# A third seven-product pair in the double gate blocks of a decoder layer, with more buffers around it and the background weight loads at other rates

## The chip, the cores and the metric

The kernel runs on one core of one Trainium2 chip. The metric is the device time of one launch in microseconds (us). TensorE (PE) multiplies 128x128 weights by 128x512 blocks, VectorE (DVE) and ScalarE (ACT) prepare operands and read results, SyncE's queue (SP) issues nearly all DMAs. PSUM has eight banks of 128x512 fp32; the kernel uses four as `acc` and four as `misc`.

## The reference

One decoder layer, T = 256 tokens, D = 2048, feed-forward width 5632, all fp32:

```python
mod = silu(c) @ w_ada + b_ada                 # shift1, scale1, gate1, shift2, scale2, gate2
h = rms_norm(x, norm1_gain) * (1 + scale1) + shift1
proj = h @ w_in                               # q, k, v of three mixers, r_gla, a_gla, gate_cols
g = sigmoid(gate_cols.reshape(b, t, 3, d))    # three branch gates of 2048 columns each
y = g[:, :, 0] * (o_sb @ w_br_sb) + g[:, :, 1] * (o_dil @ w_br_dil) + g[:, :, 2] * (o_gla @ w_br_gla)
x = x + gate1 * (y @ w_out)
h = rms_norm(x, norm2_gain) * (1 + scale2) + shift2
x = x + gate2 * swiglu(h, w_ffn_in, w_ffn_out)
```

The mixers o_sb, o_dil and o_gla (stick-breaking, dilated and gated linear attention) are small beside the weight products.

## The kernel before, in words

**Products.** Every fp32 product is made of three: the left factor and the weight are each split into a high part (rounded to fp32r) and a low remainder, and `mm3` (L172 to L175) multiplies high by high, high by low and low by high into one bank. Weights come as raw tiles of 512 KB (`raw`, L151 in `load_weights`, L216 in `load_pair`). ACT casts the high half `whi` (L165, L236), DVE subtracts it from the raw tile to give `wlo` (L166, L222). One such pair of halves is a "room". Rooms and raws are rings of four, longer where a stage gives further tags (`more_rooms`, `more_raws`); tags such as X1, A9, T0, ada are fixed pieces of SBUF used by one stage after another.

**Places.** A double block of output (two blocks of 512 columns for both halves of 128 tokens: four banks) is computed by `fast_products` in eight places, each of 256 rows of the weights. A plain place costs 8 x 3 = 24 matmuls and two splits of 128x1024 on DVE. A place marked 1 is a seven-product pair (Strassen's scheme): 7 x 3 = 21 matmuls, but DVE makes three splits of 128x1024, one of 128x512 and four differences of 128x512. It needs sums of the left factors (`sums_of_h`) and four further banks for the products that are shared between outputs. After the last fast place DVE combines those four banks (L316 to L319), and `merge` adds the combinations to the four outputs (L273).

**Stages.** After the input projection come, in order: `gate_block(0, br)` for three branches (one block of 512 gate columns each), three `gate_pair`s (double blocks 1 and 2 of the gates of each branch), the transposes of the GLA output, which stand in PE's order just ahead of the first pair and whose results are read on DVE at L1263, the `y_block`s 0 to 2 (the branch projections times the gates), the last gate blocks and `y_block(3)`, the output projection with `w_out` in four blocks n of 512 columns, and the feed-forward part. The residual of block n of the output projection loads a tile of x (L1424, `A<-x`), multiplies the bank by gate1 (L1347, which is the last reader of the bank) and adds (L1348).

**Background.** The rows of `w_ada` for later modulation vectors are streamed in meanwhile: a generator issues one load of 512 KB per step and a multiply-accumulate on DVE (L424). `tick(rate)` advances it by `rate` steps every second 128-row slice of the weights. The rates are constants at the top (`RATE_PAIRS` for the gate pairs, `RATE_Y`, `RATE_LAST`, `RATES_OP`).

**What sets the order.** The code is recorded, and a scheduler orders each engine's instructions by priorities (`prio`) and its own estimate of the times. Every engine then runs its own list strictly in that order, and waits at an instruction until its semaphores are there.

Of the kernel before, what the change touches and what calls it, by code (L numbers as in the profile page):

```python
# [10 lines left out]
F32 = mybir.dt.float32  # L11
# [6 lines left out]
P = 128  # L18
T = 256
# [10 lines left out]
N_DIL = 6  # L30
N_GLA = 4
SEG_SHIFT1, SEG_SCALE1, SEG_GATE1, SEG_SHIFT2, SEG_SCALE2, SEG_GATE2 = range(6)
RATE_IN, RATE_MID, RATE_GATES, RATE_PAIRS, RATE_Y, RATE_LAST = 0.8, 0.6, 0.65, 0.42, 0.5, 0.7

RATES_OP, RATES_FFN, RATE_OUT = (0.85, 0.5, 0.0), (0.75, 0.9, 0.7, 0.6), 0.5
GATE2_CUT = 12
LOOK = 3
DEFER = 4
# [11 lines left out]
OUT_B = ((0, 0), (1, 0)) + tuple(x for a, b in zip((8, 9, 10, 11, 12, 13, 6, 7), (2, 3, 4, 5, 14, 15, 16, 17)) for x in ((a, 1), (b, 0)))  # L50
PAIRS = ((0, 0), (1, 0), (5, 1), (2, 0), (6, 1), (7, 1), (3, 0), (4, 0))
PAIRS_4 = ((0, 0), (1, 0), (4, 1), (5, 1), (2, 0), (6, 1), (7, 1), (3, 0))
GATE_PAIRS = ((0, 0), (1, 0), (4, 1), (2, 0), (3, 0), (5, 1), (6, 0), (7, 0))
FOUR = (2, 3, 5, 6, 8)
RANK = 16
ROW_N1, ROW_N2, ROW_SBQ, ROW_SBK, ROW_DILQ, ROW_DILK, ROW_GB, ROW_GG = 16, 32, 48, 49, 50, 51, 52, 56
# [24 lines left out]
def trunk(ctx: ExitStack, tc: tile.TileContext, I, out):  # L81
# [16 lines left out]
    def S(tag, shape, dtype=F32):  # L98
        return slot.tile(shape, dtype, tag=tag, name=nm(tag))
# [101 lines left out]
    def sums_of(sf, h, a, b):  # L201

        (a0, b0), (a1, b1) = ((x[:, a, :], x[:, b, :]) for x in h)
        for dst, x, y, op in (
            (0, a1, b1, ALU.add), (2, a0, a1, ALU.subtract), (1, sf[:, 0], a0, ALU.subtract), (3, b0, sf[:, 1], ALU.subtract)
        ):
            nc.vector.tensor_tensor(sf[:, dst], x, y, op=op)

    def load_pair(src, p, c0, c1, fast, tags):


        def raw_at(c):
# [3 lines left out]
            nc.sync.dma_start(raw, src[2 * p * P : (2 * p + 2) * P, c : c + NB].rearrange("(k p) c -> p k c", p=P))  # L216
            return raw

        def sub(dst, x, y):
            chain = state.get("chain")  # L220
            with tc.issue_after(chain.ins) if chain is not None else nullcontext():
                done = nc.vector.tensor_tensor(dst, x, y, op=ALU.subtract)  # L222
            if "chain" in state:
                state["chain"] = done
            return done

        def split(src):
            n = src.shape[1]
            more_rooms = state.get("more_rooms", ())
            i = state["tiles"] = (state.get("tiles", -1) + 1) % (4 + len(more_rooms))  # L230
            if i < len(more_rooms):
                hi, lo = (S(tag, [P, 2, NB], F32R) for tag in more_rooms[i])
            else:
                hi = wp.tile([P, 2, NB], F32R, tag="whi", name=nm("whi"), bufs=4)
                lo = wp.tile([P, 2, NB], F32R, tag="wlo", name=nm("wlo"), bufs=4)
            nc.scalar.copy(hi[:, :n, :], src)  # L236
            state["split"] = sub(lo[:, :n, :], src, hi[:, :n, :].bitcast(F32))
            return [(hi[:, i, :], lo[:, i, :]) for i in range(n)]

        with prio():  # L240
            if not fast:
                return [split(raw_at(c0)), split(raw_at(c1))]
            r0, r1 = raw_at(c0), raw_at(c1)
            b11, b21 = split(r0)
            ta, tb = (S(tag, [P, 2, NB]) for tag in tags)
            sub(ta[:, 0], r1[:, 0], r0[:, 0])
            sub(ta[:, 1], r1[:, 1], r1[:, 0])
            (b22,) = split(r1[:, 1:2])
            sub(tb[:, 0], r1[:, 1], ta[:, 0])
            sub(tb[:, 1], r0[:, 1], tb[:, 0])  # L250
            t1, t3 = split(ta)
            t2, t4 = split(tb)
            return b11, b21, b22, t1, t3, t2, t4
# [955 lines left out]
                gates[1 + i, br] = g  # L1209

    def sums_of_h():
        j = 2
        full = S("X1", [P, 4, T])
        nc.vector.tensor_tensor(full, hT[0][j].bitcast(F32), hT[1][j].bitcast(F32), op=ALU.add)
        sf = S("X2", [P, 4, 2, P])
        sums_of(sf, [full[:, :, t * P : (t + 1) * P] for t in range(NT)], slice(0, 4, 2), slice(1, 4, 2))
        hi, lo = (S(tag, [P, 4, 2, P], F32R) for tag in ("T1", "T2"))
        nc.scalar.copy(hi, sf)
        nc.vector.tensor_tensor(lo, sf, hi.bitcast(F32), op=ALU.subtract)
        return {2 * j + m: [(hi[:, i, m, :], lo[:, i, m, :]) for i in range(4)] for m in range(2)}  # L1220

    with prio():
        groups = dil_weights()
# [3 lines left out]
    ring["tags"] = ("AR0", "AR1", "KC", "KD")  # L1227
    od, turns = mixture(groups[0])
    gate_block(0, 1, turns)
    gate_block(0, 2)  # L1230


# [431 lines left out]
```

## Time and profile before

| | us |
|---|---|
| median of three runs (1577.26, 1577.41, 1579.7) | 1577.41 |
| the profiled execution, its own time | 1576.77 |
| span of its trace | 1575.0 |
| granted TensorE clock in it | 0.999 |
| PE busy / DVE busy / ACT busy, of the span | 99% / 89% / 56% |

In the trace a row gives start, duration, engine, line and operation with output and inputs by the program's names; in brackets stands how long the engine had been idle and what released it. Durations of neighbouring rows overlap a little, so what an operation costs in a row of many is the distance of the starts. "PE" is the matmul and "PEld" the load of its weights, which runs beside it. In the trace the gate pairs run from 490.89 to about 620 us, the output projection from about 777 to 869 us.

### The profile page before, as it was taken

Reading aid. Unit: us, or ns where it says so; the run is one execution under the profiler, and the core shown is the slowest. Engines: PE = TensorE matmul, PEld = TensorE weight load, DVE = VectorE, ACT = ScalarE, POOL = GpSimd, SP = SyncE. Lnnn points to the kernel's source line nnn. Section 1 sums busy time; section 2 is a strip of 40 time slices with the busy share of each in tenths; the row PEclk is TensorE's granted clock in tenths of the full one; section 3 lists DMA queues with packets and bytes.
Section 4 is the critical chain, followed back from the end, with each engine's and each line's share of the span. In section 5 each row is a group of like instructions: output and inputs, shape, how many; then the busy total and the mean of one; then the engine's idle time right before and its main releaser. Section 6 shows DMA issues by size and latency. Waiting matters only on the chain.

```text
span 1575.0 us, 20266 instructions
## 1 busy us (share of the span) xinstructions
PE 1563.4 (99%) x7186; PEld 1293.5 (82%) x7186; DVE 1394.3 (89%) x1704; ACT 876.9 (56%) x1215; POOL 12.6 (1%) x24
## 2 busy tenths in 40 slices
PE   8999999999999999999999999999999999999998
PEld 7878888888888788888888888888888888888887
DVE  6889996888888899987977888999999999899896
ACT  5654448875765545444435645556555555455553
POOL 1000000000000000000000000000000000000000
PEclk9999999999999999999999999999999999999999
DMA  9999997677787888989998886665666566876764
GB/s 333 361 326 323 336 308 239 221 237 224 240 293 256 269 290 273 316 255 320 305 329 258 299 301 205 188 212 188 201 203 211 174 201 231 291 229 202 222 212 136
DMA packets 196317, 402.26 MB, mean 255 GB/s; under 512 B 13102, under 2 KB 28116, under 8 KB 196216
## 3 DMA queue, kind: packets, MB, share of 16 engines
q1 hardware_dynamic: 194952, 397.75, 76.5%
q0 software_dynamic: 1088, 3.16, 0.5%
q8 instruction: 56, 0.92, 0.2%
q14 instruction: 45, 0.37, 0.1%
q10 hardware_dynamic: 176, 0.07, 0.0%
HBM read 395.68 MB, written 5.24 MB: 255 GB/s over the span
## 4 chain that ended last, share of the span: by engine, by line
PE 91%; DVE 4%; DMA 2%; ACT 2%; issue 1%; SPq 0%; DVEq 0%; ACTq 0%
PE acc L175 21%; PE acc L174 21%; PE acc L173 21%; PE misc L174 7%; PE misc L175 7%; PE misc L173 7%; DVE wlo L222 1%; PE acc L579 1%; PE misc L948 1%; DVE A L222 1%; PE misc L1287 1%; DVE T L424 0%; DVE wlo L166 0%; DMA A<-x 0%; PE misc L572 0%
## 5 line engine op out<-in xcount | busy, mean ns | idle before, releaser
L165 ACT CAST whi<-raw 128x1024 fp32r<-128x1024 f32 (+1 forms) x277 | 278.8, 1012 | 286.5 <-PE acc L175 193.1
L166 DVE TENSOR_TENSOR wlo<-raw,whi 128x1024 fp32r<-128x1024 f32 (+1 forms) x277 | 322.0, 1171 | 93.8 <-ACT whi L165 92.5
L173 PE MATMUL acc<-whi,H 128*128 128x512 f32 x997 | 390.5, 392 | 1.2 <-ACT H L591 0.8
L174 PE MATMUL acc<-wlo,H 128*128 128x512 f32 x997 | 388.9, 390 | 0.8 <-DVE wlo L166 0.7
L175 PE MATMUL acc<-whi,H 128*128 128x512 f32 x997 | 388.8, 391 | 0.5 <-DVE H L598 0.4
L175 PEld LDWEIGHTS acc<-whi,H 128*128 128x128 f32 x997 | 187.0, 188 | 40.2 <-DVE H L598 1.4
L173 PEld LDWEIGHTS acc<-whi,H 128*128 128x128 f32 x997 | 187.2, 188 | 39.9 <-ACT H L591 1.3
L174 PEld LDWEIGHTS acc<-wlo,H 128*128 128x128 f32 x997 | 187.4, 188 | 39.2 <-DVE wlo L166 1.7
L236 ACT CAST whi<-raw 128x1024 fp32r<-128x1024 f32 (+1 forms) x130 | 125.4, 975 | 66.0 <-PE acc L175 32.7
L222 DVE TENSOR_TENSOR wlo<-raw,whi 128x1024 fp32r<-128x1024 f32 (+1 forms) x130 | 144.1, 1125 | 15.9 <-ACT whi L236 14.9
L175 PE MATMUL acc<-whi,A 128*128 128x512 f32 x221 | 86.1, 389 | 0.0
L173 PE MATMUL acc<-whi,A 128*128 128x512 f32 x210 | 82.0, 390 | 0.0
L174 PE MATMUL acc<-wlo,A 128*128 128x512 f32 x210 | 81.7, 389 | 0.0
L174 PE MATMUL misc<-wlo,H 128*128 128x512 f32 (+1 forms) x190 | 73.6, 387 | 1.3 <-DVE wlo L222 1.3
L173 PE MATMUL misc<-whi,H 128*128 128x512 f32 (+1 forms) x190 | 73.6, 387 | 0.0
L175 PE MATMUL misc<-whi,H 128*128 128x512 f32 (+1 forms) x190 | 73.5, 387 | 0.0
L222 DVE TENSOR_TENSOR A<-raw,A 128x1024 fp32r<-128x1024 f32 (+2 forms) x54 | 53.8, 1002 | 1.3 <-ACT A L236 0.8
L424 DVE SCALAR_TENSOR_TENSOR ada<-AR,csil,ada 128x1024 f32<-128x1024 f32 x39 | 49.7, 1279 | 5.1 <-DMA AR<-w_ada 5.0
L175 PEld LDWEIGHTS acc<-whi,A 128*128 128x128 f32 x221 | 41.5, 188 | 8.7
L236 ACT CAST A<-raw 128x1024 fp32r<-128x1024 f32 (+1 forms) x36 | 35.9, 1003 | 21.7 <-PE acc L175 7.2
L174 PEld LDWEIGHTS acc<-wlo,A 128*128 128x128 f32 x210 | 39.4, 188 | 8.1
L173 PEld LDWEIGHTS acc<-whi,A 128*128 128x128 f32 x210 | 39.4, 188 | 8.0
(682 smaller groups left out, 3038.3 us busy)
## 6 DMA issues: line engine op xcount, KB each, us to landing
raw<-w_in SPq DMA_DIRECT2D x192, 512.0 KB, 4.7
raw<-w_ffn_in SPq DMA_DIRECT2D x135, 512.0 KB, 4.7
raw<-w_ffn_out SPq DMA_DIRECT2D x73, 512.0 KB, 4.7
AR<-w_ada SPq DMA_DIRECT2D x62, 512.0 KB, 4.9
raw<-w_out SPq DMA_DIRECT2D x32, 512.0 KB, 5.6
OS<-w_ada SPq DMA_DIRECT2D x24, 512.0 KB, 6.1
KD<-w_ada SPq DMA_DIRECT2D x22, 512.0 KB, 5.5
AR<-w_ffn_in SPq DMA_DIRECT2D x22, 512.0 KB, 4.2
```

The source lines that it names most:

```text
L165: state["cast"] = nc.scalar.copy(hi[:, :n, :], raw[:, :n, :])
L166: state["split"] = nc.vector.tensor_tensor(lo[:, :n, :], raw[:, :n, :], hi[:, :n, :].bitcast(F32), op=ALU.subtract)
L173: nc.tensor.matmul(ps, lh, rh, start=start, stop=False, skip_group_check=seeded)
L174: nc.tensor.matmul(ps, lh, rl, start=False, stop=False, skip_group_check=seeded)
L175: state["mm"] = nc.tensor.matmul(ps, ll, rh, start=False, stop=stop, skip_group_check=seeded)
L222: done = nc.vector.tensor_tensor(dst, x, y, op=ALU.subtract)
L236: nc.scalar.copy(hi[:, :n, :], src)
L424: nc.vector.scalar_tensor_tensor(acc, raw, c, acc, op0=ALU.mult, op1=ALU.add)
L579: state["warm"] = nc.tensor.matmul(ps, ones_r, wide, start=True, stop=True)
L948: nc.tensor.matmul(ps[:n, t * N_GLA + h, :].rearrange("p (s l) -> p s l", l=L), at(f, h, t)[:, :n], odd(at(f, h, t)), start=True, stop=True,)
L1287: nc.tensor.transpose(ps[:, i, :], src[:, i * P : (i + 1) * P], ident)
```

## The change

- `GATE_PAIRS`: places 3, 5 and 7 (counted from one) are seven-product pairs; before, 3 and 6 were. So each gate pair has three fast places and five plain ones, and its last fast place is the last but one.
- The gate pairs get more rooms and raws. A room of one tag ("ada") holds both halves; the new helper `room` makes it.
- `sums_of_h` makes sums for a third pair of row blocks, and is called ahead of `gate_block(0, 2)` instead of behind it.
- The background is advanced more slowly in the gate pairs (0.25 steps instead of 0.42) and a little faster after them.

```diff
-RATE_IN, RATE_MID, RATE_GATES, RATE_PAIRS, RATE_Y, RATE_LAST = 0.8, 0.6, 0.65, 0.42, 0.5, 0.7
-RATES_OP, RATES_FFN, RATE_OUT = (0.85, 0.5, 0.0), (0.75, 0.9, 0.7, 0.6), 0.5
+RATE_IN, RATE_MID, RATE_GATES, RATE_PAIRS, RATE_Y, RATE_LAST = 0.8, 0.6, 0.65, 0.25, 0.55, 0.75
+RATES_OP, RATES_FFN, RATE_OUT = (0.85, 0.55, 0.1), (0.75, 0.9, 0.7, 0.6), 0.5
-GATE_PAIRS = ((0, 0), (1, 0), (4, 1), (2, 0), (3, 0), (5, 1), (6, 0), (7, 0))
+GATE_PAIRS = ((0, 0), (1, 0), (4, 1), (2, 0), (5, 1), (3, 0), (6, 1), (7, 0))
...
+    def room(tags):
+        if len(tags) == 1:
+            hl = S(tags[0], [P, 2, 2, NB], F32R)
+            return hl[:, 0], hl[:, 1]
+        return (S(tag, [P, 2, NB], F32R) for tag in tags)
...
     def sums_of_h():
-        j = 2
-        full = S("X1", [P, 4, T])
...
+        for p0, n, tags in ((4, 2, ("T1", "T2")), (6, 1, ("T3",))):
+            j, c = p0 // 2, slice(0, 2 * n)
...
     gate_block(0, 1, turns)
+    h_sums = sums_of_h()
     gate_block(0, 2)
...
-    h_sums = sums_of_h()
     state["rate"] = RATE_PAIRS
-    gate_pair(0, acc_bank, misc_bank, (("X1", "X2"), ("A9", "A10")), ("T3",))
-    gate_pair(1, misc_bank, acc_bank, (("A9", "A10"),), ("X2", "T3"))
-    gate_pair(2, acc_bank, misc_bank, (("A9", "A10"),), ("T3",))
+    gate_pair(0, acc_bank, misc_bank, (("X1", "X2"), ("A9", "A10"), ("ada",)), ("T0", "A8"))
+    gate_pair(1, misc_bank, acc_bank, (("A9", "A10"), ("X1", "T0"), ("ada",)), ("X2", "A8"))
+    gate_pair(2, acc_bank, misc_bank, (("A9", "A10"), ("ada",)), ("T0", "X2"))
```

Behind the added lines the line numbers are 7 to 16 higher: L222 is L229 in the changed kernel, L273 is L280, L424 is L431, L1263 is L1279, L1347 and L1348 are L1362 and L1363, L1424 is L1439.

**The GLA rows in the first gate pair, on DVE.** The GLA transposes occupy the four misc banks (names ending in a number are buffers; `misc_1004` to `misc_1009` before, `misc_1011` to `misc_1016` after), and the L1263 rows are their last readers; the first pair's shared products need those banks. Before:

```order
L1263 SCALAR_TENSOR_TENSOR A5_1003_4589<-misc_1004_4590,vec_99,A11_1002_4588 128x2x128
L1263 SCALAR_TENSOR_TENSOR A5_1003_4589<-misc_1005_4599,vec_99,A11_1002_4588 128x2x128
L1263 SCALAR_TENSOR_TENSOR A6_1007_4609<-misc_1008_4610,vec_99,A12_1006_4608 128x2x128
L222 TENSOR_TENSOR wlo_1037_4686<-A1_1031_4672,whi_1036_4685 128x1024
L1263 SCALAR_TENSOR_TENSOR A5_1003_4589<-misc_1005_4599,vec_99,A11_1002_4588 128x2x128
```

After:

```order
L229 TENSOR_TENSOR wlo_1047_4733<-T0_1045_4730,whi_1046_4732 128x1024
L229 TENSOR_TENSOR A1_1056_4775<-raw_1051_4766,A1_1056_4775 128x512
L488 TENSOR_TENSOR mod2_964_4370<-mod2_964_4370,bada_100 128x16
L431 SCALAR_TENSOR_TENSOR T4_913_4127<-AR1_1002_4497,csil_91,T4_913_4127 128x1024
L229 TENSOR_TENSOR wlo_1050_4739<-A8_1048_4736,whi_1049_4738 128x1024
L1279 SCALAR_TENSOR_TENSOR A5_1010_4610<-misc_1011_4611,vec_99,A11_1009_4609 128x2x128
L1279 SCALAR_TENSOR_TENSOR A5_1010_4610<-misc_1012_4620,vec_99,A11_1009_4609 128x2x128
L1279 SCALAR_TENSOR_TENSOR A6_1014_4630<-misc_1015_4631,vec_99,A12_1013_4629 128x2x128
L229 TENSOR_TENSOR wlo_1054_4771<-raw_1051_4766,whi_1053_4770 128x1024
L1279 SCALAR_TENSOR_TENSOR A5_1010_4610<-misc_1011_4611,vec_99,A11_1009_4609 128x2x128
L229 TENSOR_TENSOR A10_1060_4785<-A0_1055_4774,A9_1059_4784 128x1024
```

The GLA rows stand behind more splits and differences of the first two fast places than before.

**The end of the first gate pair, on DVE.** `KC`, `scr` and `T6` hold combinations of the shared banks; the rows onto `acc` are the merge adds. Before:

```order
L222 TENSOR_TENSOR wlo_1086_4901<-T3_1084_4898,whi_1085_4900 128x1024
L316 TENSOR_TENSOR KC_1087_4925<-misc_1059_4775,T6_1088_4926 128x512
L424 SCALAR_TENSOR_TENSOR T4_913_4127<-KD_1060_4798,csil_91,T4_913_4127 128x1024
L317 TENSOR_TENSOR KC_1087_4925<-misc_1057_4773,KC_1087_4925 128x512
L318 TENSOR_TENSOR scr_1089_4927<-misc_1058_4774,KC_1087_4925 128x512
L273 TENSOR_TENSOR acc_1038_4689<-acc_1038_4689,T6_1088_4926 128x512
L319 TENSOR_TENSOR KC_1087_4925<-misc_1057_4773,scr_1089_4927 128x512
L273 TENSOR_TENSOR acc_1040_4691<-acc_1040_4691,KC_1087_4925 128x512
```

After:

```order
L229 TENSOR_TENSOR wlo_1102_5015<-raw_1100_5012,whi_1101_5014 128x1024
L229 TENSOR_TENSOR A0_1113_5038<-raw_1110_5032,raw_1109_5030 128x512
L323 TENSOR_TENSOR KC_1091_4961<-misc_1065_4794,T6_1092_4962 128x512
L229 TENSOR_TENSOR A0_1113_5038<-raw_1110_5032 128x512
L324 TENSOR_TENSOR KC_1091_4961<-misc_1063_4792,KC_1091_4961 128x512
L325 TENSOR_TENSOR scr_1093_4963<-misc_1064_4793,KC_1091_4961 128x512
L280 TENSOR_TENSOR acc_1040_4698<-acc_1040_4698,T6_1092_4962 128x512
L326 TENSOR_TENSOR KC_1091_4961<-misc_1063_4792,scr_1093_4963 128x512
L280 TENSOR_TENSOR acc_1041_4699<-acc_1041_4699,scr_1093_4963 128x512
```

Before, two merge adds stood ahead of the products of the last place, which add to the same banks behind them; now all four stand behind the last place, among the splits of the next pair.

**The output projection, on SP, DVE and PE.** On SP, around the tiles of x. Before, `raw_1606` is the first weight tile of block n = 2:

```order
L151 DMA raw_1592_7271<-w_out 128x2x512
L151 DMA raw_1606_7401<-w_out 128x2x512
L1424 DMA A2_1519_7000<-x 128x2x512
L151 DMA raw_1609_7407<-w_out 128x2x512
L1424 DMA A3_1520_7002<-x 128x2x512
```

After, `raw_1612` is the first of block n = 2, and `raw_1630` the seventh:

```order
L151 DMA raw_1624_7436<-w_out 128x2x512
L151 DMA raw_1627_7442<-w_out 128x2x512
L527 DMA KC_1636_7473<-w_ada 128x1024
L151 DMA raw_1630_7448<-w_out 128x2x512
L1439 DMA A2_1528_7023<-x 128x2x512
```

On DVE, before (`acc_1524` is the second bank of block n = 0):

```order
L166 TENSOR_TENSOR wlo_1591_7268<-raw_1589_7265,whi_1590_7267 128x1024
L1348 TENSOR_TENSOR A2_1519_7000<-A2_1519_7000,scr_1564_7215 128x512
L1347 TENSOR_TENSOR scr_1566_7220<-T4_913_4127,acc_1524_7009 128x512
L166 TENSOR_TENSOR wlo_1594_7274<-raw_1592_7271,whi_1593_7273 128x1024
L1348 TENSOR_TENSOR A2_1519_7000<-A2_1519_7000,scr_1566_7220 128x512
```

After (`acc_1533` is that bank now, `wlo_1620` and `wlo_1623` are the third and the fourth split of block n = 2):

```order
L166 TENSOR_TENSOR wlo_1620_7427<-raw_1618_7424,whi_1619_7426 128x1024
L166 TENSOR_TENSOR wlo_1623_7433<-raw_1621_7430,whi_1622_7432 128x1024
L1363 TENSOR_TENSOR A2_1528_7023<-A2_1528_7023,scr_1566_7210 128x512
L1362 TENSOR_TENSOR scr_1568_7215<-T4_913_4127,acc_1533_7032 128x512
L1363 TENSOR_TENSOR A2_1528_7023<-A2_1528_7023,scr_1568_7215 128x512
```

On PE at the start of block n = 2, before (`acc_1604` and `acc_1605` are its two banks):

```order
L173 MATMUL acc_1604_7399<-whi_1607_7403,A9_1289_5882 128x512
L174 MATMUL acc_1604_7399<-wlo_1608_7404,A9_1289_5882 128x512
L175 MATMUL acc_1604_7399<-whi_1607_7403,A10_1290_5883 128x512
L173 MATMUL acc_1605_7400<-whi_1607_7403,A9_1289_5882 128x512
L174 MATMUL acc_1605_7400<-wlo_1608_7404,A9_1289_5882 128x512
L175 MATMUL acc_1605_7400<-whi_1607_7403,A10_1290_5883 128x512
```

After (`acc_1610` and `acc_1611` are the two banks; with four acc banks in turn, `acc_1611` is the bank that `acc_1533` was):

```order
L173 MATMUL acc_1610_7410<-whi_1622_7432,A0_1333_6084 128x512
L174 MATMUL acc_1610_7410<-wlo_1623_7433,A0_1333_6084 128x512
L175 MATMUL acc_1610_7410<-whi_1622_7432,A1_1334_6085 128x512
L173 MATMUL acc_1611_7411<-whi_1613_7414,A9_1292_5891 128x512
L174 MATMUL acc_1611_7411<-wlo_1614_7415,A9_1292_5891 128x512
```

The tiles of x are now loaded and added one block later, and PE starts block n = 2 with 24 products into its first bank alone, where before the two banks took turns three products at a time.

More of the change, by code (lines that the diff above doesn't have):

```diff
@@ L231, in split @@
             if i < len(more_rooms):
-                hi, lo = (S(tag, [P, 2, NB], F32R) for tag in more_rooms[i])
+                hi, lo = room(more_rooms[i])
             else:
@@ L1211, in sums_of_h @@
     def sums_of_h():
-        j = 2
-        full = S("X1", [P, 4, T])
[L1214 to L1220, printed above, removed]
+        out = {}
+        for p0, n, tags in ((4, 2, ("T1", "T2")), (6, 1, ("T3",))):
+            j, c = p0 // 2, slice(0, 2 * n)
+            full = S("X1", [P, 4, T])[:, c]
+            nc.vector.tensor_tensor(full, hT[0][j][:, c].bitcast(F32), hT[1][j][:, c].bitcast(F32), op=ALU.add)
+            sf = S("X2", [P, 4, 2, P])[:, :, :n]
+            sums_of(sf, [full[:, :, t * P : (t + 1) * P] for t in range(NT)], slice(0, 2 * n, 2), slice(1, 2 * n, 2))
+            if n == 2:
+                hi, lo = (S(tag, [P, 4, n, P], F32R) for tag in tags)
+            else:
+                hl = S(tags[0], [P, 2, 4, n, P], F32R)
+                hi, lo = hl[:, 0], hl[:, 1]
+            nc.scalar.copy(hi, sf)
+            nc.vector.tensor_tensor(lo, sf, hi.bitcast(F32), op=ALU.subtract)
+            for m in range(n):
+                out[p0 + m] = [(hi[:, i, m, :], lo[:, i, m, :]) for i in range(4)]
+        return out
     with prio():
```

## The prediction

> **What bounds the kernel now.** I read the page first: its busy times and the chain that ended last.
>
> ```profile
> span 1575.0 us, 20266 instructions
> PE 1563.4 (99%) x7186; PEld 1293.5 (82%) x7186; DVE 1394.3 (89%) x1704; ACT 876.9 (56%) x1215; POOL 12.6 (1%) x24
> PE 91%; DVE 4%; DMA 2%; ACT 2%; issue 1%; SPq 0%; DVEq 0%; ACTq 0%
> ```
>
> PE sets the time: it is busy nearly throughout and holds 91% of the chain. A change can gain only by taking products from PE or by removing moments in which PE waits; anything on DVE, ACT or SP counts only where it makes PE wait. So the next view is the busy time in windows, one for each gate pair (PE, PEld, DVE, ACT in this order).
>
> ```profile
> 491.00:534.00 43.00, 42.66 (x189) 35.01 (x188) 40.36 (x49) 22.34 (x29) 0.00 (x0) 1.00 0.86 284
> 534.00:577.00 43.00, 41.72 (x184) 34.16 (x183) 40.07 (x45) 24.26 (x29) 0.00 (x0) 1.00 0.82 268
> 577.00:620.00 43.00, 43.00 (x192) 35.61 (x191) 41.27 (x45) 22.48 (x26) 0.00 (x0) 1.00 0.82 270
> ```
>
> DVE works 40 to 41 of 43 us here: it idles 2.6, 2.9 and 1.7 us a pair. The groups of PE's waits between 491 and 620 us, and behind 620 us, say what PE waits for:
>
> ```profile
> PE misc L174 <- DVE wlo L222: 1.3, 1, 1.3
> PE acc L173 <- DVE acc L273: 0.3, 1, 0.3
> PE misc L1370 <- DVE ada L1358: 0.2, 1, 0.2
> ```
>
> Two waits in the gate pairs, and only 0.2 us in the whole rest. So the stage of the change holds nearly all that is to be had in waits.
>
> **Products on PE.** The timeline of PE near the end of the first pair, with the DVE row that released it:
>
> ```profile
> 526.15 0.39 PE L175 MATMUL acc<-A,H 128*128 128x512 f32 x1
> 527.51 0.39 PE L175 MATMUL acc<-A,H 128*128 128x512 f32 x1
> 528.25 0.47 PE L173 MATMUL acc<-whi,H 128*128 128x512 f32 x1 [0.34 <-DVE acc L273]
> 528.55 0.39 PE L174 MATMUL acc<-wlo,H 128*128 128x512 f32 x1
> 527.41 0.69 DVE L273 TENSOR_TENSOR acc<-acc,T 128x512 f32<-128x512 f32 x1
> ```
>
> Products last 0.39 us but overlap: six start between 526.15 and 527.51, so one costs 0.227 us. A third fast place takes 24 - 21 = 3 products from each of three pairs: 9 x 0.227 = **-2.04 us**. PE does little else in these pairs, so all of it lies on the path.
>
> **The two waits.** From 527.51 to 528.25 are 0.74 us in place of 0.227, and to the next 0.30: a loss of 0.51 + 0.07 = 0.59 us. The last place's first product waits for a merge add in the middle of the pair. After the change no product follows a merge into the same banks (the rows of the pair's end in the change section): this wait is gone. What could be late instead is the hand-over of the four shared banks to the next pair. They are complete a place earlier, 24 products or 5.4 us ahead of its start, and DVE reads them out in eight rows or fewer; the next pair needs the last of them only after 18 products of its own. I cost that at nothing, covered by about 9 us. The other wait, in the second pair, on DVE, SP and PE:
>
> ```profile
> 541.86 0.37 SPq L216 DMA_DIRECT2D X<-w_in  x1
> 541.70 1.28 DVE L424 SCALAR_TENSOR_TENSOR T<-AR,csil,T 128x1024 f32<-128x1024 f32 x1
> 542.90 0.68 DVE L222 TENSOR_TENSOR A<-raw,A 128x512 f32<-128x512 f32 x1
> 543.50 1.22 DVE L222 TENSOR_TENSOR wlo<-A,whi 128x1024 fp32r<-128x1024 f32 x1
> 546.25 0.69 DVE L222 TENSOR_TENSOR A<-X 128x512 f32<-128x512 f32 x1 [1.54 <-DMA X<-w_in]
> 546.86 1.22 DVE L222 TENSOR_TENSOR wlo<-A,whi 128x1024 fp32r<-128x1024 f32 x1
> 548.00 1.28 DVE L424 SCALAR_TENSOR_TENSOR T<-KD,csil,T 128x1024 f32<-128x1024 f32 x1
> 549.28 0.69 DVE L222 TENSOR_TENSOR A<-X,raw 128x512 f32<-128x512 f32 x1
> 549.89 1.22 DVE L222 TENSOR_TENSOR wlo<-T,whi 128x1024 fp32r<-128x1024 f32 x1
> 549.48 0.40 PE L173 MATMUL misc<-whi,H 128*128 128x512 f32 x1
> 551.16 0.50 PE L174 MATMUL misc<-wlo,H 128*128 128x512 f32 x1 [1.28 <-DVE wlo L222]
> 551.50 0.40 PE L175 MATMUL misc<-whi,H 128*128 128x512 f32 x1
> ```
>
> DVE stands 1.54 us at a difference whose raw tile was issued only at 541.86; the split that PE needs next stands behind it. PE loses 1.68 - 0.227 = 1.45, and 0.11 to the next product: 1.56 us. With a raw more and two rooms more this tile is loaded earlier, and one multiply-accumulate fewer stands there. Sum of both: **-2.15 us**, with 0 and -2.15 as ends.
>
> **DVE's load in a pair.** By the starts above, a split of 1024 costs 1.14 (546.86 to 548.00), an operation of 512 costs 0.60, a multiply-accumulate 1.20. A plain place is 2 x 1.14 = 2.28, a fast one 3 x 1.14 + 5 x 0.60 = 6.42, merging 8 x 0.60 = 4.8. Before: 6 x 2.28 + 2 x 6.42 + 4.8 + 20/3 x 1.20 = 39.3 of PE's 186 x 0.227 = 42.2 us. After: 5 x 2.28 + 3 x 6.42 + 4.8 + 4 x 1.20 = 40.3 of 183 x 0.227 = 41.5 us. It fits, with 1.2 us left a pair, if the deeper rings keep DVE's own waits short. Following the changed lists by these costs, every split comes 2.4 us or more ahead of its product. The earlier sums of the left factors cost DVE some 2 us in a stage where PE doesn't wait: nothing. The eight multiply-accumulates that leave the pairs (8 x 1.20 = 9.6 us of DVE, and their loads on SP) lie later beside PE's work, where only 0.2 us of waits are seen: nothing, with 0 to 0.5.
>
> **The GLA rows in the first pair.** They are few and short:
>
> ```profile
> L1263 DVE SCALAR_TENSOR_TENSOR A<-misc,vec,A x8: 473/474/478, 495.7 to 503.7; 128x256 fp32r<-128x256 f32 x8
> 490.89 0.47 PE L173 MATMUL acc<-whi,H 128*128 128x512 f32 x1
> ```
>
> After the change the first product into a misc bank is the 62nd of the pair, due at 490.89 + 61 x 0.227 = 504.7, and waits for the fifth GLA row, behind a split whose room PE leaves with the 48th product, at about 501.9. Cast and split take 2.3 us (804.45 to 806.77 below), the GLA row 0.4: 504.6 to 505.2. The other banks follow as closely. I take **+0.4 us**, between 0 and 2.
>
> **The tile of x in the output projection.** This is the new wait. The chain as the trace has it, on ACT, DVE, SP and PE, with the landing times of the x tiles and of others in this stage:
>
> ```profile
> 804.45 1.05 ACT L165 CAST whi<-raw 128x1024 fp32r<-128x1024 f32 x1 [1.67 <-PE acc L175]
> 805.54 1.23 DVE L166 TENSOR_TENSOR wlo<-raw,whi 128x1024 fp32r<-128x1024 f32 x1 [1.50 <-ACT whi L165]
> 806.79 0.37 SPq L151 DMA_DIRECT2D raw<-w_out  x1
> 807.21 0.46 SPq L1424 DMA_DIRECT2D A<-x  x1
> 814.34 0.69 DVE L1348 TENSOR_TENSOR A<-A,scr 128x512 f32<-128x512 f32 x1 [2.14 <-DMA A<-x]
> 814.95 0.68 DVE L1347 TENSOR_TENSOR scr<-T,acc 128x512 f32<-128x512 f32 x1
> 817.86 0.39 PE L173 MATMUL acc<-whi,A 128*128 128x512 f32 x1
> 820.82 1.06 ACT L165 CAST whi<-raw 128x1024 fp32r<-128x1024 f32 x1 [1.66 <-PE acc L175]
> DMA to landing us min/median/max: 6.9/7.0/7.0
> raw<-w_out SPq DMA_DIRECT2D x30, 512.0 KB, 5.6
> KD<-w_ada SPq DMA_DIRECT2D x4, 512.0 KB, 7.6
> ```
>
> PE leaves a room; ACT casts the next tile into it, DVE splits it, the end of the split lets SP issue a raw tile and behind it `A<-x`; 9.89 us after the cast's start (804.45 to 814.34) DVE adds x, and only then multiplies the bank by gate1 (L1347), which frees it. Before, the bank's next products were far off. After the change the same chain hangs on the third split of block n = 2. Call the start of that block N. Its room is left 12 products ahead, at N - 2.72; the cast follows 0.24 later (PE's places change every 2.72 us, at 817.86 and so at 820.58; the cast starts at 820.82), at N - 2.48. L1363 then starts at N + 7.41, L1362 at N + 8.02 and ends at N + 8.70; PE sees it 0.15 later (528.10 to 528.25 above), at N + 8.85. PE's order puts 24 products into the first bank ahead, so its first product into the freed bank is due at N + 5.44: it waits **3.4 us**, and all later products with it. Behind the waiting L1363 stands also the fifth split of the block, but its product comes 24 products after the stall, so that costs no more. Ends: with a landing like the weights' 5.6 us the wait is 2.0 us, with 7.6 us it is 4.0; it is nothing only below 3.6 us. All four x tiles landed within 6.9 to 7.0, so I take 3.4.
>
> [...]
>
> **The sum.** -2.04 - 2.15 + 0.4 + 3.4 = -0.4 us. The profiled execution took 1576.77 us, 1.8 outside its span, and 0.6 below the median; the change applied to it gives 1576.4, to the median 1577.0.
>
> **The rivals.**
> *The x tile costs nothing*, since it lands early enough or the stall is given back by shorter waits behind it. For: SP and the DMA engines have the stalled time to catch up. Against: four of four landings. -2.04 - 2.15 + 0.4 = -3.8: 1573.6 us. Chance 0.24.
> *DVE becomes the bound in the gate pairs.* If DVE goes on idling for its inputs as it did (2.6, 2.9, 1.7, a mean of 2.4 us a pair), it needs 40.3 + 2.4 = 42.7 us for 41.5 of PE, and PE stalls 1.2 us in each pair; with 2 us more of late casts, since ACT serves three fast places now, up to 2. That decides as soon as the waits pass the spare 1.2 us. Three pairs of 1.2 to 2 are 3.6 to 6, on top of the sum: 1580.6 to 1583.0, say 1581.5. For: DVE's 97% load. Against: the deeper rings take away just these waits. Chance 0.22.
> *The change doesn't take effect*: the waits are replaced by equal ones at the same places. Then -2.04 + 0.4 + 3.4 = +1.8: 1579.2, chance 0.1.
>
> **How the numbers follow.** The forecast, with a landing of 5.6 to 7.6, has 0.44. About 0.2% (3.2 us) is what a measurement of this kernel can tell from no change, so faster begins below 1574.3 and slower above 1580.6. Faster is the first rival, 0.24; slower nearly all of the second, 0.22; within are the forecast and the third, 0.54. The likeliest is 1577.0 us, for itself between 1575.5 and 1577.8. The range takes in the first rival whole and the second to its nearer half: 1573.3 to 1581.3.
>
> **What would show it.** Right: nine products fewer; no wait longer than 0.6 us in the three pairs, which end 3.5 to 4.2 us earlier against their start; then one wait of PE of about 3.4 us, released by L1362, 24 products into block n = 2, behind an `A<-x` that landed after some 7 us. Wrong: that wait is absent or under 1 us (faster), or the gate pairs show waits for L229 splits of over 1 us each (slower).

## The result, and the profile after

The changed kernel takes **1580.79 us** (median of 16 runs, 1578.99 to 1583.28), the kernel before 1576.81 us on the same chip (16 runs, 1575.53 to 1579.70). The ratio is 1.0024, interval 1.0017 to 1.0031: a loss of 4.0 us, where the forecast was 1577.0 and no measurable change. The profiled execution took 1581.39 us with a span of 1579.6, 4.6 us more than before.

The page's lines on the span, the busy times and the chain that ended last, of the changed kernel:

```profile
span 1579.6 us, 20268 instructions
PE 1564.1 (99%) x7177; PEld 1292.0 (82%) x7177; DVE 1407.4 (89%) x1728; ACT 879.7 (56%) x1222; POOL 12.6 (1%) x24
PE 85%; DVE 6%; ACT 3%; DMA 3%; issue 2%; POOL 0%; SPq 0%; ACTq 0%; DVEq 0%; POOLq 0%
```

PE has nine products fewer (7177 for 7186), as the change says. But PE's share of the chain falls from 91% to 85%, and DVE's, ACT's and the DMAs' grow: PE waits more. DVE is busy 13 us longer. The list of what PE waited for from 480 us to the end (us in total, times, longest) names the places:

```profile
PE acc L173 <- DVE scr L1362: 2.7, 1, 2.7
PE acc L174 <- DVE wlo L166: 0.8, 1, 0.8
PE misc L1137 <- DVE T L1132: 0.7, 1, 0.7
PE misc L173 <- DVE A L334: 0.5, 1, 0.5
PE acc L173 <- DVE T L334: 0.3, 1, 0.3
...
```

The two waits that the kernel before had in its gate pairs are gone; five others stand in these lines. A wait in this list is shorter than what PE loses by it (2.7 against 2.83 us at L1362, below), and a slow clock does not show in it at all (1.50 us behind that wait). So I also took, for each matmul, the distance from its start to the next start, less the median of that distance for matmuls of its shape, and summed these losses by stage:

| us lost by PE | before | after | difference |
|---|---|---|---|
| gate pairs (500 to 600) | 2.12 | 0.48 | -1.64 |
| last gate blocks (700 to 750) | 0.06 | 1.13 | +1.07 |
| output projection, block n = 2 (800 to 850) | -0.07 | 4.57 | +4.64 |
| its block n = 3 and behind (850 to 900) | 1.01 | 2.15 | +1.14 |
| feed-forward part (1000 to 1200) | 0.45 | 1.89 | +1.44 |
| all else | 15.76 | 15.66 | -0.10 |
| sum | 19.33 | 25.88 | +6.55 |

With -2.04 for nine products this is +4.5 us, and the spans differ by 4.6: nothing is left over.

**The gate pairs.** The windows of the three pairs (PE, PEld, DVE, ACT), and the rows at the GLA hand-over in the first:

```profile
491.00:534.00 43.00, 42.87 (x190) 34.94 (x188) 40.83 (x52) 25.38 (x34) 0.00 (x0) 1.00 0.78 255
534.00:577.00 43.00, 43.00 (x191) 35.63 (x190) 42.29 (x48) 22.32 (x27) 0.00 (x0) 1.00 0.80 260
577.00:620.00 43.00, 43.00 (x192) 35.60 (x191) 41.44 (x48) 23.97 (x29) 0.00 (x0) 1.00 0.68 218
...
504.82 0.39 PE L173 MATMUL acc<-whi,H 128*128 128x512 f32 x1
505.33 0.47 PE L173 MATMUL misc<-X,H 128*128 128x512 f32 x1
```

PE is full in the second and third pair. DVE works 42.3 of 43 us in the second, and PE still waits for nothing. The only losses are at the first products into the misc banks: 505.33 - 504.82 = 0.51 in place of 0.227 and 0.08 to the next one, and 0.17 at the next bank (509.09 to 509.71), 0.53 us in all.

**The tile of x.** SP's, DVE's and PE's rows in block n = 2, and the landing time of the four x tiles:

```profile
820.73 0.46 SPq L1439 DMA_DIRECT2D A<-x  x1
DMA to landing us min/median/max: 6.7/6.7/6.7
827.42 0.69 DVE L1363 TENSOR_TENSOR A<-A,scr 128x512 f32<-128x512 f32 x1 [4.41 <-DMA A<-x]
828.02 0.68 DVE L1362 TENSOR_TENSOR scr<-T,acc 128x512 f32<-128x512 f32 x1
825.71 0.39 PE L175 MATMUL acc<-whi,A 128*128 128x512 f32 x1
828.76 0.80 PE L173 MATMUL acc<-whi,A 128*128 128x512 f32 x1 [2.67 <-DVE scr L1362]
829.36 0.63 PE L174 MATMUL acc<-wlo,A 128*128 128x512 f32 x1
829.78 0.63 PE L175 MATMUL acc<-whi,A 128*128 128x512 f32 x1
...
832.43 0.40 PE L174 MATMUL acc<-wlo,A 128*128 128x512 f32 x1
```

The predicted wait is there, at its place and with its releaser: 828.76 - 825.71 - 0.227 = 2.83 us. But the products behind it last 0.63 us instead of 0.39, and start 0.42 apart instead of 0.227 (829.36, 829.78). The windows around it show why (PEclk, the granted clock, is the third number from the end):

```profile
825.21:828.63 3.42, 0.89 (x4) 0.38 (x3) 1.21 (x2) 0.49 (x1) 0.00 (x0) 1.00 1.04 395
828.63:832.04 3.41, 3.28 (x9) 2.59 (x10) 2.06 (x4) 1.23 (x5) 0.57 (x1) 0.50 0.67 264
832.04:835.46 3.42, 3.42 (x18) 2.86 (x17) 3.06 (x5) 2.75 (x5) 0.00 (x0) 1.00 0.03 11
```

The clock falls to 0.50 at 828.63, just before PE starts again, and is back at 1.00 after 3.41 us. In the trace of the kernel before it stays at 1.00 from 6.65 to 1573.36 us.

**What follows in block n = 3.** SP's waits between 824 and 836 us, its next issue, and the rows of ACT and PE at the first late weight:

```profile
SPq L151 <- DVE wlo L166: 10.3, 1, 10.3
834.85 7.12 SPq L151 DMA_DIRECT2D raw<-w_out  x5
848.35 1.05 ACT L165 CAST T<-raw 128x1024 fp32r<-128x1024 f32 x1 [2.65 <-DMA raw<-w_out]
851.25 0.39 PE L173 MATMUL acc<-whi,A 128*128 128x512 f32 x1
852.46 0.50 PE L174 MATMUL acc<-wlo,A 128*128 128x512 f32 x1 [0.81 <-DVE wlo L166]
```

While DVE stands at x and PE stands behind it, no split frees a raw, and SP issues no load of w_out for over 10 us. The tiles of block n = 3 land late, and PE loses 852.46 - 851.25 - 0.227 = 0.98 us more. That the wait at x brings this loss is not shown: run 3 below has the wait without the loss, and runs 5, 8 and 12 have such a loss (0.81, 0.99 and 1.82 us) without the wait.

**The remaining two places.** PE at the broadcast of gate1 in the last gate blocks, at a hand-over in the feed-forward part, and the window of that part before and after (two kernels, before first):

```profile
729.77 0.39 PE L173 MATMUL acc<-whi,H 128*128 128x512 f32 x1
730.87 0.39 PE L1137 MATMUL misc<-T,ones_r 128*128 128x256 f32 x1 [0.70 <-DVE T L1132]
1025.15 0.39 PE L174 MATMUL acc<-A,H 128*128 128x512 f32 x1
1026.03 0.47 PE L173 MATMUL misc<-whi,AR 128*128 128x512 f32 x1 [0.50 <-DVE A L334]
...
960.00:1045.00 85.00, 85.00 (x384) 70.53 (x383) 81.01 (x100) 48.70 (x57) 0.00 (x0) 1.00 0.61 197
960.00:1045.00 85.00, 84.50 (x382) 69.85 (x381) 82.81 (x102) 48.75 (x56) 1.06 (x2) 1.00 0.65 207
```

DVE is at 95% of this window before and at 97% after. What is more in it are two multiply-accumulates at its start (965.92 and 974.73 us), where the kernel before has none; from 1000 to 1200 us neither kernel has any, and DVE is busy 194.8 us before and 195.0 after. Bank hand-overs in that stretch that came in time before now cost PE 0.4 and 0.7 us.

### The profile page after: what moved, and what is told of

Read it like the earlier page. It is cut to its first block, busy times and chain, and to the rows that moved or that the text cites. A ratio compares the mean times of both kernels' runs of the same rounds, so it can differ in the third digit from the quotient of the medians.

```text
span 1579.6 us, 20268 instructions
## 1 busy us (share of the span) xinstructions
PE 1564.1 (99%) x7177; PEld 1292.0 (82%) x7177; DVE 1407.4 (89%) x1728; ACT 879.7 (56%) x1222; POOL 12.6 (1%) x24
## 4 chain that ended last, share of the span: by engine, by line
PE 85%; DVE 6%; ACT 3%; DMA 3%; issue 2%; POOL 0%; SPq 0%; ACTq 0%; DVEq 0%; POOLq 0%
PE acc L175 20%; PE acc L174 20%; PE acc L173 20%; PE misc L173 7%; PE misc L175 7%; PE misc L174 7%; DVE wlo L229 1%; ACT whi L165 1%; DVE wlo L166 1%; DVE OD L229 1%; PE acc L586 1%; PE misc L955 1%; DVE KD L229 1%; DMA raw<-w_in 1%; PE misc L1303 0%
## 5 line engine op out<-in xcount | busy, mean ns | idle before, releaser
L229 DVE TENSOR_TENSOR wlo<-raw,whi 128x1024 fp32r<-128x1024 f32 (+1 forms) x130 | 144.8, 1134 | 13.9 <-ACT whi L243 12.9
L173 PE MATMUL misc<-whi,H 128*128 128x512 f32 (+1 forms) x209 | 81.0, 388 | 0.0
L175 PE MATMUL misc<-whi,H 128*128 128x512 f32 (+1 forms) x209 | 80.9, 387 | 0.0
L174 PE MATMUL misc<-wlo,H 128*128 128x512 f32 (+1 forms) x209 | 80.9, 387 | 0.0
L431 DVE SCALAR_TENSOR_TENSOR ada<-AR,csil,ada 128x1024 f32<-128x1024 f32 x38 | 48.2, 1280 | 6.0 <-DMA AR<-w_ada 6.0
L243 ACT CAST whi<-OD 128x1024 fp32r<-128x1024 f32 (+1 forms) x25 | 25.5, 1020 | 40.7 <-DVE OD L229 21.8
L229 DVE TENSOR_TENSOR A<-raw,A 128x512 f32<-128x512 f32 (+2 forms) x53 | 47.2, 898 | 0.7 <-ACT A L243 0.2
```

Of the source, the lines that this page charges most:

```text
L173: nc.tensor.matmul(ps, lh, rh, start=start, stop=False, skip_group_check=seeded)
L174: nc.tensor.matmul(ps, lh, rl, start=False, stop=False, skip_group_check=seeded)
L175: state["mm"] = nc.tensor.matmul(ps, ll, rh, start=False, stop=stop, skip_group_check=seeded)
L431: nc.vector.scalar_tensor_tensor(acc, raw, c, acc, op0=ALU.mult, op1=ALU.add)
```

## The experiments

The theory after this reading: the third pair is worth its 2 us and the two gate-pair waits are gone, but the background steps that went out of the pairs bring an x tile late, with a slow clock behind it, and waits in stages where DVE is nearly full. The rival: what PE waits for is set by DVE's and SP's work as a whole, and a wait that is removed in one place comes back in another. All medians, with the ratio to the kernel before on the same chip:

| kernel | median us (runs) | ratio, 95% interval |
|---|---|---|
| changed | 1580.79 (16) | 1.0024 (1.0017 to 1.0031) |
| x tiles early | 1582.61 (8) | 1.0031 (1.0021 to 1.0042) |
| changed, old rates | 1581.39 (12) | 1.0023 (1.0015 to 1.0032) |
| before, new rates alone | 1579.73 (12) | 1.0015 (1.0006 to 1.0023) |
| products in the wait | 1583.86 (6) | 1.0037 (1.0023 to 1.0050) |
| x tiles in mid-block | 1579.07 (11) | 1.0013 (1.0004 to 1.0022) |
| the same, GLA rows ahead | 1577.65 (12) | 1.0007 (0.9999 to 1.0016) |
| x mid-block, rings at 0 | 1576.64 (11) | 0.9999 (0.9990 to 1.0008) |
| all three | 1576.37 (11) | 0.9995 (0.9986 to 1.0003) |
| before, rings at 5 | 1576.92 (11) | 0.9998 (0.9990 to 1.0007) |
| old rates, two rows ahead | 1578.14 (11) | 1.0009 (1.0000 to 1.0017) |
| the same, rings at 0 | 1578.69 (12) | 1.0011 (1.0002 to 1.0019) |
| x mid-block, rings at 0, two fast places | 1578.74 (11) | 1.0007 (0.9998 to 1.0016) |

Runs of one kernel differ by 3 to 8 us, and a profile is one of them; so the medians decide, and the traces say where.

**1. The x tiles ordered early.**

```diff
-        nc.sync.dma_start(xr, I["x"][...])
+        with prio():
+          nc.sync.dma_start(xr, I["x"][...])
```

> The changed kernel with one edit: the loads of the x tiles for the output projection are issued with priority, so that on SP they stand ahead of the first weight tiles of block n = 0; the order of everything up to there is unchanged. Theory (the loss is the late x tile): the wait on L1362 in block n = 2 (2.83 us), the products at half clock behind it (1.74 us) and the late weights of block n = 3 that follow (1.09 us) all go, 5.7 us: about 1575.1 us, a ratio to before of 0.999. Rival (the x tiles take the same DMA time wherever they stand, and push the first weight tiles of the output projection back): the wait only moves to the start of the output projection, about 1579 to 1581 us.

The wait for L1362 is gone, and the time is not better. At the start of the output projection PE now waits for its first weights, and a slow stretch follows (PE's rows; the clock is at 0.50 from 779.14 to 782.55 us):

```profile
777.48 0.73 PE L173 MATMUL acc<-whi,A 128*128 128x512 f32 x2 [1.94 <-ACT whi L165]
778.74 0.50 PE L174 MATMUL acc<-wlo,A 128*128 128x512 f32 x1 [0.53 <-DVE wlo L166]
```

Two 512 KB loads of x now stand on SP just ahead of the first weights, which are issued at 771.00 us instead of 761.07. PE loses 4.76 us there (750 to 800). The rival held in kind, and the time is above its 1579 to 1581.

**2. The changed kernel with the old rates.**

```diff
-RATE_IN, RATE_MID, RATE_GATES, RATE_PAIRS, RATE_Y, RATE_LAST = 0.8, 0.6, 0.65, 0.25, 0.55, 0.75
+RATE_IN, RATE_MID, RATE_GATES, RATE_PAIRS, RATE_Y, RATE_LAST = 0.8, 0.6, 0.65, 0.42, 0.5, 0.7
-RATES_OP, RATES_FFN, RATE_OUT = (0.85, 0.55, 0.1), (0.75, 0.9, 0.7, 0.6), 0.5
+RATES_OP, RATES_FFN, RATE_OUT = (0.85, 0.5, 0.0), (0.75, 0.9, 0.7, 0.6), 0.5
```

> The changed kernel with the background rates of before: three fast places and deeper rings stay. Theory (the later background displaces the x tiles): SP's order again has the first x tile right behind the first weight tile of block n = 2, so the wait on L1362 and the half clock are gone, -5.7 us; but DVE has 20/3 multiply-accumulates a pair again, 43.5 us of work for 41.5 of PE, so the gate pairs wait up to 2 us each: 1575 to 1581 us, with the wait in the gate pairs and none in block n = 2. Rival (the third pair alone causes the wait in block n = 2): the wait is still there and the time is 1581 us or more.

The x wait and the feed-forward waits are gone, and the time stays. The waits that the theory put into the gate pairs are not there beyond the GLA rows: neither of the two waits of before is in PE's list, with the old rates too. The first lines of PE's list from 480 us, the rows of its longest wait on PE, ACT and DVE, and the window behind it:

```profile
PE misc L1137 <- DVE T L1132: 2.1, 1, 2.1
PE misc L173 <- DVE A L1279: 1.4, 1, 1.4
661.05 0.39 PE L175 MATMUL acc<-whi,A 128*128 128x512 f32 x1
663.57 0.39 PE L1137 MATMUL misc<-T,ones_r 128*128 128x256 f32 x1 [2.13 <-DVE T L1132]
651.11 0.42 ACT L1131 CAST T<-T 128x256 fp32r<-128x256 f32 x1
663.10 0.41 DVE L1132 TENSOR_TENSOR T<-T,T 128x256 fp32r<-128x256 f32 x1
664.30:667.60 3.30, 3.30 (x10) 2.59 (x9) 2.53 (x4) 1.12 (x3) 0.00 (x0) 0.52 0.95 340
```

The cast for the broadcast of gate1 is done at 651.5, but its difference (L1132) stands at 663.10 in DVE's list, behind 11 us of splits, sums and multiply-accumulates. Again the clock is low (0.52 in the 3.3 us shown) behind the wait. The old rates cost about what the new ones do, in another place.

**3. The kernel before with the new rates alone.** (The two RATE lines of the diff, nothing else.)

> The kernel before with nothing but the new rates: two fast places, the old rings. Theory: the x tiles stand behind the seventh weight tile of block n = 2 again and the same wait appears, 2.8 us and 1.7 us at half clock and 1.1 us in block n = 3: about 1582 us, a ratio of 1.003 to 1.004; the wait of 1.6 us in the second gate pair may go, which would give 1581. Rival (the rates are harmless, the third pair and the rings cause the loss): 1576.8 us, a ratio of 1.000.

This alone costs 1.0015 (1.0006 to 1.0023), 1579.73 us, between the theory's 1582 and the rival's 1576.8. The same x wait appears, without the third pair, and so do feed-forward waits (0.59 and 0.53 us lost). The gate-pair waits of before vanish too, without any new room or raw: 500 to 600 loses -0.15 us in place of 2.12. PE's rows at the x tile, and the window from the middle of the wait on:

```profile
826.07 0.39 PE L175 MATMUL acc<-whi,A 128*128 128x512 f32 x1
828.41 0.50 PE L173 MATMUL acc<-whi,A 128*128 128x512 f32 x1 [1.95 <-DVE scr L1347]
...
830.58 0.39 PE L174 MATMUL acc<-wlo,A 128*128 128x512 f32 x1
826.67:830.08 3.41, 1.67 (x8) 1.36 (x9) 2.58 (x4) 1.45 (x4) 0.57 (x1) 1.00 0.91 304
```

The wait is 2.11 us and no slow stretch follows. From the released product to the last row shown are 830.58 - 828.41 = 2.17 us here, and for the same instructions in the same order 832.43 - 828.76 = 3.67 in the changed kernel: the slow clock costs 1.50 us.

**4. Products in the wait.** The changed kernel with 12 further matmuls, whose results nobody reads, put into PE's wait in block n = 2.

```diff
...
+                    for _ in range(12):
+                        last = nc.tensor.matmul(state["fill_ps"], ones_r, state["fill_by"], start=True, stop=True)
...
```

> The changed kernel with twelve useless products into a free bank in PE's order ahead of the first product of the second bank of block n = 2, where PE waits; the wait itself stays. Theory (the half clock behind the wait comes from PE's idleness): PE is busy for 2.7 us of the wait, the products behind it cost 0.227 us each from the first on, 1.7 us less: about 1579.1 us. Rival (the slow stretch comes from something else at that place, the DMA traffic or the PSUM bank): the products behind the wait still cost 0.43 us each, 1580.8 us.

PE's window from 820 us on:

```profile
820.00:829.00 9.00, 9.00 (x43) 7.46 (x42) 3.93 (x6) 2.03 (x2) 0.00 (x0) 1.00 0.91 311
829.00:835.00 6.00, 6.00 (x27) 4.90 (x27) 4.03 (x7) 2.46 (x7) 0.65 (x2) 1.00 0.67 241
```

Same place, the same late tile, no idle PE, and the clock stays at 1.00, which fits PE's idleness as what brings the slow stretch; since run 3 kept its clock with an idle PE, this one trace doesn't prove it. The time is higher, not lower: 1583.86 us against the theory's 1579.1. The fill takes 12 x 0.227 = 2.72 us itself in place of the wait, and waits at other places are longer in this run: the late weights at 836.60 and 852.61 cost 0.87 and 1.66, the GLA rows 1.35, a feed-forward hand-over 1.40. Why they are isn't shown.

**5. The x tiles in mid-block.** The load of tile n (0 to 2) stands with the seventh weight slice of block n; it has about a block's time until it is read.

```diff
...
-        nc.sync.dma_start(xr, I["x"][...])
+        if n == 3:
+            nc.sync.dma_start(xr, I["x"][...])
...
+    def x_load(n):
+        nc.sync.dma_start(x2[n], I["x"][...])
...
-        block(pss, y_at, I["w_out"], 0, KC, n * NB)
+        block(pss, y_at, I["w_out"], 0, KC, n * NB, steps={6: lambda: x_load(n)})
```

In `I["x"][...]` the indices are left out.

> The changed kernel; the loads of the x tiles 0, 1 and 2 are issued in the middle of the blocks n = 0, 1 and 2 of the output projection, neither ahead of its first weight tiles (as with the early x tiles) nor behind the seventh weight tile of n = 2. Theory (each PE wait costs its own length, and beyond about 2 us the half clock too): no wait on L1362 and none at the start of the output projection, no half clock, no late weights in n = 3: 5.7 us less than the changed kernel's profiled run, about 1575.5 us, a ratio to before of 0.999. Rival (the output projection is short of DMA time whatever the order): a wait of over 1 us stays somewhere in it, 1578 us or more.

No wait on x, no slow stretch; 1.0013 (1.0004 to 1.0022), 1.7 us below the changed kernel by medians, and well above the theory's 1575.5. In the profiled run PE still loses 1.07 us from 800 to 850, most of it at a late weight of block n = 3, 1.64 around the GLA rows and 2.40 in the feed-forward part. The time is the rival's (1578 or more), though no wait of over 1 us stays in the output projection.

**6. The same, with the GLA rows ordered ahead on ACT and DVE.**

```diff
+            with prio():
                 for par in range(2):
                     ...
```

> As with the x tiles in the middle of the blocks, and the GLA casts and L1279 rows have priority, so that on DVE they stand ahead of the differences of the second fast place. Theory: the wait of the first gate pair (0.4 to 1.6 us in the runs so far) goes, 1574.0 to 1575.0 us. Rival (DVE has no room there, the splits behind them come late instead): the wait moves to a split of the first pair, no change against the kernel with the x tiles in the middle.

The GLA loss is gone (500 to 550: -0.07). The median falls by 1.4, to 1577.65 instead of the theory's 1574 to 1575, and the two ratios' intervals overlap. The feed-forward waits are larger in this run than in run 5 (3.8 us of losses from 1000 to 1200).

**7. x in mid-block, and the rings set to 0 behind the gate pairs.** Since the pairs now have longer rings, they leave the counters of rooms and raws at 5, where before they stood at 0. Only the fast places use these counters, so it shows next in the feed-forward part, whose rings are eight rooms and six raws long at first: its first fast place starts at another room and another raw.

```diff
+    state["tiles"], state["raws"] = 0, 0
     state["rate"] = RATE_Y
```

> As with the x tiles in the middle of the blocks, and the counters of the rooms and raws are set to 0 behind the gate pairs, which is where they stood there before the change (the change leaves them at 5 and 5). Theory (the waits of 0.3 to 1.4 us at L173 in the feed-forward part near 1025, 1154 and 1193 us come from the shifted phase of the rings): they go back to the 0.2 and 0.1 us of before, 1.0 to 1.8 us less: about 1574.5 us. Rival (they come from the background's later steps): they stay, 1575.5 us.

2.4 us less than run 5, by a line that changes no work (the two ratios' intervals overlap a little, but the same line also takes 1.3 us from run 6 to run 8); the theory's 1574.5 is not reached. PE's list from 480 us is down to two entries:

```profile
PE misc L173 <- DVE A L1279: 1.0, 1, 1.0
PE misc L1386 <- DVE ada L1374: 0.4, 1, 0.4
```

The feed-forward part loses 0.44 us, as before the change.

**8. All three.**

> The three edits together: x tiles in the middle of the blocks, GLA rows with priority, ring counters as before. Theory: only the nine products fewer, the two waits of the gate pairs that went (2.04 + 2.15 us) and small waits are left: 4 us less than before, about 1573 us, a ratio of 0.9975. Rival (the gains do not add up, since DVE at 97% gives a wait back somewhere in the pairs): a ratio of 0.999 or more.

0.9995 (0.9986 to 1.0003): 4.4 us below the changed kernel, and not to be told from the kernel before. In its trace the GLA wait is gone, but 0.99 us is lost at a late weight of w_out and 2.5 in the feed-forward part. The gains of 6 and 7 do not add: the rival held, and the theory's 1573 failed.

**9. The kernel before, rings at 5.**

> The kernel before, with one thing of the changed one: the rings of raw and weight tiles stand at 5 behind the gate pairs instead of at 0. Theory (the phase of the rings makes the feed-forward waits): waits of DVE L334 of together 0.7 to 1.6 us appear between 1000 and 1200 us, where before has 0.2, and the time is 1577.5 to 1579. Rival (the later background steps make them): the feed-forward part stays as before and so does the time, 1576.8, within 0.1%.

0.9998 (0.9990 to 1.0007), and no feed-forward waits. So the position of the rings makes no feed-forward waits by itself; only together with the new rates does it matter. It doesn't decide alone there: runs 3 and 8 have the rings at 0, and lose 1.36 and 2.52 us from 1000 to 1200.

**10. Old rates, with the two waits of run 2 ordered ahead.** (`prio()` around L1131 and L1132 and around the GLA rows, L1279, which the expectation calls sums of left factors.)

> The changed kernel with the old background rates, and with two places ordered ahead on their engines: the sums of left factors of the gate pairs' first half (L1279), and the split behind the gate broadcast (L1131, L1132). Theory (those two waits are all that the old rates cost: 1.2 and 4.3 us of the 1581 measured with the old rates): the third pair's 2.0 and the two waits' 2.1 are then left over, and the time is 1573 to 1575, ratio 0.9975 to 0.999. Rival (in a stretch where DVE is nearly full a wait that is pushed away comes back at the next hand-over): the waits reappear at other lines of PE's list, 576 to 578, ratio 0.999 or more. (By 576 and 578 are meant 1576 and 1578 us.)

The rival held: neither wait is there any more, and PE waits elsewhere, mostly at lines that had been in time in run 2 (its list from 480 us; the last row was 1.0 there):

```profile
PE misc L173 <- ACT T L1139: 2.4, 1, 2.4
PE acc L174 <- DVE wlo L166: 1.0, 2, 0.8
PE misc L174 <- DVE wlo L166: 0.7, 1, 0.7
```

PE loses 5.3 us from 600 to 700, where the kernel before loses nothing.

**11. The same, rings at 0.**

> The run above with the rings of raw and weight tiles set back to 0 behind the gate pairs. Theory of the phase: as with the old rates the feed-forward part shows almost no waits at phase 5 already (0.2 us), the phase changes nothing here, and the time is that of the run above within 0.1%. Rival: the phase alone is worth 1 to 2 us again, as it was with the new rates and the x tiles in the middle (2.4 us).

0.03% apart from run 10: here the phase is worth nothing, as expected. The wait is again elsewhere (a split of w_br at 622 us, 2.47 us, with the clock at 0.50 from 623.05 to 626.46).

**12. Run 7 with two fast places.**

```diff
-GATE_PAIRS = ((0, 0), (1, 0), (4, 1), (2, 0), (5, 1), (3, 0), (6, 1), (7, 0))
+GATE_PAIRS = ((0, 0), (1, 0), (4, 1), (2, 0), (3, 0), (5, 1), (6, 0), (7, 0))
```

> The kernel of the run with the x tiles in the middle and the rings at 0 (1576.64 us), with the old GATE_PAIRS: only the third fast place is taken back, everything else of the change stays (rooms, raws, sums, rates). Theory (nine products on a full PE are worth their 2.04 us): PE has 9 products more, the gate pairs show no waits as with the rates alone, the time is 1578.7, ratio about 1.001. Rival (DVE has 1.0 us a pair less to do, 3 us in all, and other waits shrink by as much, so that the third pair is worth nothing): 1576 to 1577, ratio 0.9995 to 1.0.

2.1 us more by medians; 1.6 after the difference of the kernel before on the two chips (1577.28 and 1576.79 us). That agrees with the 2.04, but the two ratios' intervals overlap, and this run's trace has a wait of its own in block n = 3, so it supports the size and doesn't prove it:

```profile
847.78 0.50 PE L173 MATMUL acc<-whi,A 128*128 128x512 f32 x1
849.83 0.50 PE L174 MATMUL acc<-wlo,A 128*128 128x512 f32 x1 [1.54 <-DVE wlo L166]
846.94:850.36 3.42, 1.77 (x7) 0.95 (x6) 3.42 (x5) 2.20 (x3) 0.00 (x0) 1.00 0.82 268
850.36:853.77 3.41, 3.41 (x9) 2.63 (x9) 2.98 (x4) 2.06 (x4) 0.53 (x1) 0.50 0.84 252
```

## Why the prediction was wrong

The measured 1580.79 lies 3.8 above the forecast, and the interval of the ratio excludes that nothing changed; it is also above the line from which the prediction calls the kernel slower (1580.6). That it lies inside the range is luck: the range reaches to 1581.3 for the rival in which DVE stalls PE in the gate pairs, and that did not happen. Step by step:

- **Products, -2.04: right.** There are nine fewer in the trace, and with 2.04 us for them the losses and the spans add up. Run 12 gives 1.6 to 2.1, which supports it.
- **The two waits in the gate pairs, -2.15: right.** They are gone, and the pairs together lose 1.64 us less, with the GLA term in it. Of the causes given more than one is enough: run 3 has the old rings and only fewer multiply-accumulates, runs 2 and 10 have the old rates with the new rings and the new order, and in none of them is either wait left.
- **GLA rows, +0.4: right in this trace (0.53), partly by luck.** The other kernels with the third pair and these rows in their old order lose 1.25 to 1.74 us from 500 to 550.
- **The x tile, +3.4: right in place, chain and wait, but the step "so that costs no more" failed.** The wait was 2.83, within its ends, with a landing of 6.7. Behind it came 1.50 us of slow clock, which the sum did not have; with the slow restart of PE the term was 4.64 us in this run. Another 1.14 us went in block n = 3. With the old rates (runs 2, 10 and 11) only 0.2 of it is there, but the x wait isn't its cause by itself, as runs 3, 5, 8 and 12 show.
- **"The eight multiply-accumulates that leave the pairs ... lie later beside PE's work ...: nothing, with 0 to 0.5" failed.** Few waits before were read as much room. Four of the eight come to stand from 870 to 1000 us (18 for 14), where DVE is busy 38.8 of the last 40 us instead of 36.4, and the feed-forward part behind them lost 1.44 us more with the same load on DVE. That these losses come from the rates is shown by runs 2 (old rates: none) and 3 (new rates alone: 1.15 from 1000 to 1100, at other hand-overs); that the rings' position bears on them too, by runs 5, 7 and 9. How a few operations more ahead of it make DVE late at a hand-over is argued, not shown. The wait at L1137 (0.97 with the product behind it) reached this size in no other kernel with the new rates; what let it happen in this run stays open.
- **The rival in which DVE becomes the bound in the pairs** did not happen there. With the old rates (runs 2, 10, 11) a loss of the size it named came, 5.3 to 5.6 us, but behind the pairs, from 600 to 700 us.
- **The rival in which the x tile costs nothing, 1573.6,** is refuted as a sum: with the x wait gone, the GLA rows in time and the rings reset (run 8) the kernel reaches 1576.37, no more than parity.

So the sum was wrong by what it left out: 1.50 + 1.14 + 1.07 + 1.44 = 5.2 us of losses against an x wait 0.6 shorter than forecast.

What stays open is why run 8 does not come out some 4 us ahead. The runs show that in this kernel a removed wait mostly returns at another hand-over of DVE or SP (1, 4, 8, 10, 11). That DVE's 13 us of further work is the common cause fits them, but it is not shown: no run here took work off DVE alone.

## What to carry to other kernels

Few waits in a stage say that its feeder is in time, not that it has room: look at the feeder's busy share (95% here) before costing moved work at nothing. A long wait of PE must be costed with what can come behind it: here the slow clock added 1.50 us to a wait of 2.83. After a change of ring lengths, look where the rings stand for the next stage: one line was worth 1.3 to 2.4 us by medians with the new rates, and nothing with the old ones.

## What the hardware showed

The clock fell behind waits of 2.83 (changed), 2.47 (run 11), 2.29 (run 2), 2.10 and 0.69 (run 1) and 1.82 us (run 12, just behind another of 0.27), and did not behind 2.52 (run 10) and 2.11 us (run 3). In the stretches shown products then started 0.42 to 0.43 us apart for about 3.4 us. So the length of a wait alone does not decide it.

What goes with the falls can be read from PE's rows and, for the changed kernel and the one before, from the clock records of their traces. The slow stretch of the changed kernel lasts 3.413 us. The clock stands at 1.00 for 822.61 us ahead of it and for 747.52 behind it, and for 1566.72 us in the kernel before: 241, 219 and 459 times 3.413, to within 0.2 us. In the 3.41 us ahead of each fall PE started 3 to 5 matmuls, where products in a row make 15 (3.41 / 0.227; the counts in the windows shown above also have those that had begun earlier). But in the 3.41 us ahead of the end of the waits in runs 10 and 3 it started 3 and 5 as well, and the clock stayed at 1.00 there (657 to 697 us in run 10, 826.67 to 830.08 in run 3). So few starts in such a stretch do not decide it alone either. Whether it matters where a wait lies against the multiples of 3.413 us is not shown. The slow stretch may be one reason why runs of one kernel differ; one trace of each can't show it.
